# Gates of a hybrid encoder trunk: two of four contraction chunks as 2x2 Strassen products instead of one

## The chip, the cores and the metric

The kernel runs on one core of one Trainium2 chip. The metric is the device time of the whole launch in microseconds (us), the median of the runs. One execution was also recorded by the profiler; its trace is what the rows below come from. The engines are called PE (TensorE, matmuls), DVE (VectorE), ACT (ScalarE), POOL (GpSimd) and SP (SyncE, which only issues DMAs here).

## The reference, cut to what matters

Two layers of an encoder with 256 tokens and a width of 2048, all in float32. In each layer three attention branches are projected to 2048 columns and merged by sigmoid gates that are computed from the layer's input `x`:

```
ga, gb, gc = jnp.split(jax.nn.sigmoid(x @ w_gate[l] + b_gate[l]), 3, axis=-1)
mix = ga * (ya @ w_br_a[l]) + gb * (yb @ w_br_b[l]) + gc * (yc @ w_br_c[l])
x = layer_norm(DEEPNORM_ALPHA * x + mix @ w_out[l], ...)
f_gate, f_up = jnp.split(x @ w_ffn_in[l], 2, axis=-1)
x = layer_norm(DEEPNORM_ALPHA * x + (silu(f_gate) * f_up) @ w_ffn_out[l], ...)
```

`w_gate[l]` is 2048 x 6144. The change concerns the product `x @ w_gate[l]` only.

## The kernel before, in words

Every operand of a matmul is split into a high and a low part (`h`, `l`) of a reduced format, and every product of two float32 tiles is made of three matmuls, `h*wh`, `h*wl` and `l*wh`, each of 128 x 128 against 128 x 512, which accumulate in one PSUM bank. Weights come in *units*: 256 rows by 512 columns (two k tiles of 128 rows), 512 KB, loaded by SP into one of five buffers called `raw`. `split_unit` (L72 to L81) makes `wh` on ACT (L78) and then `wl` on DVE (L80), into six buffers each. The `raw` buffer is free once L80 has read it.

A plain `gemm` computes one block of 512 output columns for both halves of the tokens: a unit feeds 12 matmuls. `pair_gemm` (L317) computes two column blocks, `n1` and `n2`, at once, for the two token halves, with seven PSUM banks named `p1, p2, p3, p6, p7, q4, q5`. Four of them (`p3, q5, p7, q4`) come from the pool `psA` of four banks, which the plain gemms use too; three come from the pool `psX`. The contraction of 2048 has four chunks of 512 rows; each is done in one of these ways:

- `four(kt, c0)`: one unit of one column block, two products into two banks, 12 matmuls. A chunk takes four of them, 48 matmuls and four splits.
- `seven(c, fill)`: the chunk is a 2x2 block product by Strassen's method (Winograd's form). It loads four units (`hub`, `w22`, `w11`, `w21`), makes sums of them on DVE (L381, L389, L390, L403, each 128 x 1024) and does seven products of two k tiles each (`p7, p3, p1, q5, p6, p2, q4`), 42 matmuls and seven splits: those of `w22`, `w11`, `w21`, of the sum `hub`, and of the sum `u` three times. `fill` says which `four` calls stand between its products.

The sums on the token side are made once per layer by `x_sums` (L276) and reused by all pairs: for a `four` chunk one difference of 128 x 512 (L301) and one split, for a `seven` chunk four differences of 128 x 256 (L294, L295, L296, L298) and two splits. Their results live in twelve tiles named in `sum_tiles`, of which the gates use ten.

At the end of a pair (L452 to L467), DVE combines the seven banks and the bias of the gate (`bg`, loaded by POOL into a `raw` buffer) into four gate tiles; each of these operations is 128 x 512. Per layer the gates have six steps, three branches by two column pairs. The first step uses plain gemms; the other five call `pair_gemm`. Behind each come two plain gemms of the branch projection (eight k tiles each for branch a, four each for b and c) and on DVE L701, or L703 and L704, which multiply by the gate and add into `mix`.

The same `pair_gemm` serves the feed-forward layer, with `FF = ("7", "74", "4", "4")`, where `74` is a chunk of which half the rows go through seven products (`seven_half`).

The order of the work on each engine is fixed when the program is built, from the program's order and from the builder's own estimates; each engine then works through its list in order and waits on semaphores. In this list work of a later step can stand ahead of work of an earlier one.

Of the kernel before, what the change touches and what calls it, by code (L numbers as in the profile page):

```python
# [33 lines left out]
def trunk_kernel(ctx: ExitStack, tc: tile.TileContext, x, w_in, sinks, lq1, lk1, lq2, lk2, diff_g,  # L34
# [26 lines left out]
    def block(src, k0, c0):  # L61
        return src[k0 * P:(k0 + UK) * P, c0:c0 + CW].rearrange("(k p) n -> p k n", p=P)

    def load_raw(src, k0, c0):
        raw = wpool.tile([P, UK, CW], F32, tag="raw", name="raw", bufs=5)
        nc.sync.dma_start(raw, block(src, k0, c0))
        return raw
# [4 lines left out]
    def split_unit(raw):  # L72
        h = wpool.tile([P, UK, CW], F32R, tag="wh", name="wh", bufs=6)
        l = wpool.tile([P, UK, CW], F32R, tag="wl", name="wl", bufs=6)
        n = raw.shape[1]
        a, v = behind.pop(0) if behind else (None, None)
        with tc.issue_after(a) if a else nullcontext():
            nc.scalar.copy(h[:, 0:n], raw)  # L78
        with tc.issue_after(v) if v else nullcontext():
            split_ins.append(nc.vector.tensor_sub(l[:, 0:n], raw, h[:, 0:n].bitcast(F32)).ins)  # L80
        return h, l  # L81
# [128 lines left out]
    for layer in range(DEPTH):  # L210
# [106 lines left out]
        def pair_gemm(src, n1, n2, sums, kinds, load_bias=None, hubs=()):  # L317
# [19 lines left out]
            def prod(k, lhs, w, js=range(UK)):  # L337
                for i, j in enumerate(js):
                    (ah, al), (wh, wl) = lhs(i), w
                    nc.tensor.matmul(bank[k], ah, wh[:, j, :], start=k not in begun, stop=False)  # L340
                    begun.add(k)
                    nc.tensor.matmul(bank[k], ah, wl[:, j, :], start=False, stop=False)  # L342
                    todo[k] -= 1
                    nc.tensor.matmul(bank[k], al, wh[:, j, :], start=False, stop=todo[k] == 0)  # L344

            def part(h, l, j0):
                return lambda j: (h[:, j0 + j, :], l[:, j0 + j, :])

            def four(kt, c0):
                c, j0 = kt // 4, kt % 4  # L350
                a1, a2 = (part(xh[c][t], xl[c][t], j0) for t in range(NT))
                w = load_unit(src, kt, c0)
                if c0 == n2:
                    prod("q5", a2, w)
                    prod("p3", part(*sums[c][-1], j0 if kinds[c] == "4" else 0), w)
                else:
                    prod("p2", a1, w)
                    prod("q4", a2, w)
                units.append(w)
                if len(units) == 2:  # L360
                    run_later()
# [3 lines left out]
            def seven(c, fill):  # L365
                k1, k2 = 4 * c, 4 * c + 2
                a11, a12, a22 = (part(xh[c][t], xl[c][t], j) for t, j in ((0, 0), (0, 2), (1, 2)))
                s1, s2, s3, s4 = [part(h, l, j) for h, l in sums[c] for j in (0, 2)]

                def fours(i):  # L370
                    for f in fill[i]:
                        four(*f)

                if hubs:
                    hub = act.tile([P, UK, CW], F32, tag=hubs[c // 2], name="hub")
                    nc.sync.dma_start(hub, block(src, k1, n2))
                else:
                    hub = load_raw(src, k1, n2)
                w22 = load_raw(src, k2, n2)
                u = scr.tile([P, UK, CW], F32, tag="att", name="u", bufs=2)  # L380
                nc.vector.tensor_add(u, hub, w22)  # L381
                fours(0)
                prod("p7", s3, split_unit(u))
                prod("p3", s4, split_unit(w22))
                w11 = load_raw(src, k1, n1)
                if hubs:
                    nc.gpsimd.dma_start(hub, block(src, k1, n1), accum_op=ALU.add)
                else:
                    nc.vector.tensor_add(hub, hub, w11)  # L389
                nc.vector.tensor_add(u, u, w11)  # L390
                fours(1)
                prod("p1", a11, split_unit(w11))
                fours(2)
                if not hubs:
                    prod("q5", s1, split_unit(hub))
                    fours(3)
                prod("p6", s2, split_unit(u))
                w21 = load_raw(src, k2, n1)
                if hubs:
                    nc.gpsimd.dma_start(u, block(src, k2, n1), accum_op=ALU.add)  # L400
                    fours(3)
                else:
                    nc.vector.tensor_add(u, u, w21)  # L403
                fours(4)
                prod("p2", a12, split_unit(w21))
                if hubs:
                    prod("q5", s1, split_unit(hub))
                fours(5)
                prod("q4", a22, split_unit(u))
                fours(6)  # L410

            def seven_half(fill):
                b11, b12, b22 = (part(xh[1][t], xl[1][t], j) for t, j in ((0, 0), (0, 1), (1, 1)))
                s1, s2, s3, s4 = [part(*sums[1][0], j) for j in range(4)]
                w2 = load_raw(src, 4, n2)
                w1 = load_raw(src, 4, n1)
                u = scr.tile([P, 3, CW], F32, tag="att", name="u", bufs=2)
                nc.vector.tensor_add(u[:, 0], w2[:, 0], w1[:, 0])
                nc.vector.tensor_add(w2[:, 0], w2[:, 0], w2[:, 1])
                w = split_unit(w2)  # L420
                prod("p7", s3, w, (0,))
                prod("p3", s4, w, (1,))
                nc.vector.tensor_add(u[:, 1], u[:, 0], w2[:, 1])
                w = split_unit(w1)
                prod("p1", b11, w, (0,))
                prod("p2", b12, w, (1,))
                nc.vector.tensor_add(u[:, 2], u[:, 1], w1[:, 1])
                four(*fill[0])
                w = split_unit(u[:, 0:2])
                prod("q5", s1, w, (0,))  # L430
                prod("p6", s2, w, (1,))
                four(*fill[1])
                w = split_unit(u[:, 2:3])
                prod("q4", b22, w, (0,))

            N2, N1 = ([(k, c) for k in range(4, 16, 2)] for c in (n2, n1))
            if kinds[1] == "74":
                seven(0, [N2[1:2], N2[2:3], [], N2[3:4], [], [], []])
                seven_half(N2[4:])
                for f in N1[1:]:  # L440
                    four(*f)
            elif kinds[2] == "7":
                seven(0, [N2[0:1], N2[1:2], [], [], N2[4:5], N1[0:1], []])
                seven(2, [N2[5:6], N1[1:2], [], [], [], N1[4:], []])
            else:
                seven(0, [N2[0:1], N2[1:2], N2[2:3], N2[3:4], N2[4:], N1[0:1], N1[1:2]])
                if load_bias:
                    bias = load_bias()
                for f in N1[2:]:
                    four(*f)  # L450
# [208 lines left out]
        ys = [y0, y1, y2, y3]  # L659


        GATE = ("7", "4", "4", "4")
        FF = ("7", "74", "4", "4")
        mix = [[None] * NT for _ in range(NCH)]
        mixT = [None] * NCH
# [1 line left out]
        for b, (wbr, nk, y0i) in enumerate(((w_br_a, 8, 0), (w_br_b, 4, 2), (w_br_c, 4, 3))):  # L667
# [4 lines left out]
            for c0 in range(0, NCH, 2):  # L672
                cols = [b * D + c * CW for c in (c0, c0 + 1)]

                def load_bias(cols=cols):
                    t = wpool.tile([P, 2, CW], F32, tag="raw", name="bg", bufs=5)
                    for i, c in enumerate(cols):
                        nc.gpsimd.dma_start(t[:, i], b_gate[layer][c:c + CW].partition_broadcast(P))
                    return t[:, 0], t[:, 1]

                if b == 0 and c0 == 0:
                    bgs = load_bias()
                    side.append(x_sums(sums, GATE, 0))
                    gates = []
                    for c, bg in zip(cols, bgs):
                        acc = gemm(w_gate[layer], 0, 16, c, x_lhs)
                        gates.append([tmp("gate") for _ in range(NT)])
                        for t in range(NT):
                            nc.vector.tensor_add(gates[-1][t], acc[t], bg)
                    drain()  # L690
                else:
                    gates = pair_gemm(w_gate[layer], *cols, sums, GATE, load_bias)
                for gs in gates:
# [176 lines left out]
```

## Time and profile before

| | |
|---|---|
| median of 3 runs | 2802.61 us (2802.1 to 2805.56) |
| time of the profiled execution | 2802.2 us |
| its span, first to last instruction | 2800.4 us |
| PE busy | 2770.8 us, 99% |
| DVE busy | 2086.7 us, 75% |
| ACT busy | 1376.8 us, 49% |
| granted TensorE clock, mean | 0.999 |

Busy time is the time in which an engine works at least one instruction. Consecutive instructions overlap a little, so the mean duration of one is longer than the step from one start to the next. Between the span and the execution's time lie 1.8 us.

### The profile page before, as it was taken

What the parts mean: (1) busy time and instruction counts of PE and PEld (TensorE: products, weight loads), DVE (VectorE), ACT (ScalarE), POOL (GpSimd) and SP (SyncE); (2) the same over time, 40 slices, a digit from 0 to 9 for tenths busy, and PEclk for the clock granted to TensorE, in tenths of its full rate; (3) what the DMA queues carried; (4) which work ended last, traced back from release to release, by engine and by line L of the source; (5) the groups of instructions that cost most, each with busy time, mean ns of one, the idle gap of its engine ahead of it and who ended that gap; (6) DMA issues with size and microseconds to landing.
All of it is one profiled execution on the core that took longest, in us unless ns stands there. A gap on an engine that the chain in (4) does not pass through costs nothing. (4 is left out here: it accounts for less than half of the span.)

```text
span 2800.4 us, 33958 instructions
## 1 busy us (share of the span) xinstructions
PE 2770.8 (99%) x12600; PEld 2288.2 (82%) x12600; DVE 2086.7 (75%) x2438; ACT 1376.8 (49%) x1760; POOL 60.3 (2%) x110
## 2 busy tenths in 40 slices
PE   8999999999999999999999999999999999999998
PEld 7888888887888888888878888888878888888886
DVE  6665877776996698588676568787679957985886
ACT  4545544443554455455445455444435544553552
POOL 0000000000000000000000000000000000000000
PEclk9999999999999999999999999999999999999999
DMA  7556565674656566557564555666746655665573
GB/s 250 173 158 188 164 219 188 215 254 155 210 186 213 189 191 216 190 188 232 192 211 151 180 186 182 196 204 220 242 145 218 200 201 187 199 209 189 186 239 128
DMA packets 282663, 549.22 MB, mean 196 GB/s; under 512 B 19840, under 2 KB 21376, under 8 KB 282496
## 3 DMA queue, kind: packets, MB, share of 16 engines
q1 hardware_dynamic: 276096, 526.07, 57.7%
q0 software_dynamic: 6400, 20.98, 2.9%
q8 instruction: 99, 1.62, 0.2%
q14 instruction: 68, 0.56, 0.1%
HBM read 542.78 MB, written 4.19 MB: 195 GB/s over the span
## 5 line engine op out<-in xcount | busy, mean ns | idle before, releaser
L78 ACT CAST wh<-raw 128x1024 fp32r<-128x1024 f32 x992 | 1038.9, 1053 | 1192.2 <-PE acc L117 554.3
L80 DVE TENSOR_TENSOR wl<-raw,wh 128x1024 fp32r<-128x1024 f32 x992 | 1201.0, 1221 | 508.1 <-ACT wh L78 505.3
L115 PE MATMUL acc<-wh,rh 128*128 128x512 f32 x1216 | 475.3, 391 | 0.0
L117 PE MATMUL acc<-wh,rl 128*128 128x512 f32 x1216 | 473.8, 390 | 0.0
L116 PE MATMUL acc<-wl,rh 128*128 128x512 f32 x1216 | 473.4, 389 | 0.0
L115 PE MATMUL acc<-wh,xh 128*128 128x512 f32 x768 | 307.2, 401 | 0.0
L116 PE MATMUL acc<-wl,xh 128*128 128x512 f32 x768 | 300.7, 392 | 3.6 <-DVE wl L80 1.9
L117 PE MATMUL acc<-wh,xl 128*128 128x512 f32 x768 | 300.9, 392 | 0.0
L342 PE MATMUL q<-wl,xh 128*128 128x512 f32 x720 | 280.3, 389 | 2.6 <-DVE wl L80 2.6
L340 PE MATMUL q<-wh,xh 128*128 128x512 f32 x720 | 280.3, 389 | 0.0
L344 PE MATMUL q<-wh,xl 128*128 128x512 f32 x720 | 280.1, 389 | 0.0
L117 PEld LDWEIGHTS acc<-wh,rl 128*128 128x128 f32 x1216 | 228.3, 188 | 47.3
L115 PEld LDWEIGHTS acc<-wh,rh 128*128 128x128 f32 x1216 | 228.3, 188 | 46.8
L116 PEld LDWEIGHTS acc<-wl,rh 128*128 128x128 f32 x1216 | 228.3, 188 | 46.7
L340 PE MATMUL p<-wh,sums 128*128 128x512 f32 x560 | 218.1, 389 | 0.7 <-DVE v L703 0.7
L344 PE MATMUL p<-wh,sums 128*128 128x512 f32 x560 | 218.0, 389 | 0.0
L342 PE MATMUL p<-wl,sums 128*128 128x512 f32 x560 | 217.9, 389 | 0.0
L340 PE MATMUL p<-wh,xh 128*128 128x512 f32 x480 | 188.4, 392 | 0.0
L344 PE MATMUL p<-wh,xl 128*128 128x512 f32 x480 | 186.9, 389 | 0.0
L342 PE MATMUL p<-wl,xh 128*128 128x512 f32 x480 | 186.8, 389 | 0.0
L116 PEld LDWEIGHTS acc<-wl,xh 128*128 128x128 f32 x768 | 144.5, 188 | 34.2 <-DVE wl L80 4.1
L117 PEld LDWEIGHTS acc<-wh,xl 128*128 128x128 f32 x768 | 144.2, 188 | 31.6 <-DVE xl L55 1.3
(208 smaller groups left out, 3110.1 us busy)
## 6 DMA issues: line engine op xcount, KB each, us to landing
raw<-in_w_ffn_in_dram SPq DMA_DIRECT2D x352, 512.0 KB, 4.3
raw<-in_w_gate_dram SPq DMA_DIRECT2D x192, 512.0 KB, 4.4
raw<-in_w_ffn_out_dram SPq DMA_DIRECT2D x176, 512.0 KB, 3.7
raw<-in_w_in_dram SPq DMA_DIRECT2D x144, 512.0 KB, 3.8
raw<-in_w_out_dram SPq DMA_DIRECT2D x64, 512.0 KB, 4.3
raw<-in_w_br_a_dram SPq DMA_DIRECT2D x32, 512.0 KB, 4.7
raw<-in_w_br_b_dram SPq DMA_DIRECT2D x16, 512.0 KB, 5.6
raw<-in_w_br_c_dram SPq DMA_DIRECT2D x16, 512.0 KB, 5.4
```

What stands on the lines that cost most here:

```text
L78: nc.scalar.copy(h[:, 0:n], raw)
L80: split_ins.append(nc.vector.tensor_sub(l[:, 0:n], raw, h[:, 0:n].bitcast(F32)).ins)
L115: nc.tensor.matmul(acc[t], ah, wh[:, j, :], start=kt == 0, stop=False)
L116: nc.tensor.matmul(acc[t], ah, wl[:, j, :], start=False, stop=False)
L117: nc.tensor.matmul(acc[t], al, wh[:, j, :], start=False, stop=kt == nk - 1)
L340: nc.tensor.matmul(bank[k], ah, wh[:, j, :], start=k not in begun, stop=False)
L342: nc.tensor.matmul(bank[k], ah, wl[:, j, :], start=False, stop=False)
L344: nc.tensor.matmul(bank[k], al, wh[:, j, :], start=False, stop=todo[k] == 0)
```

## The change

`GATE` names how each of the four chunks of the contraction is done in the gates. Chunk 2 becomes a `seven` as well. `pair_gemm` then takes its middle branch, in which the `fill` lists hold the remaining eight `four` calls, and the bias of the gate is loaded between the two `seven` calls instead of behind the first.

```
             elif kinds[2] == "7":
                 seven(0, [N2[0:1], N2[1:2], [], [], N2[4:5], N1[0:1], []])
+                if load_bias:
+                    bias = load_bias()
                 seven(2, [N2[5:6], N1[1:2], [], [], [], N1[4:], []])
             else:
                 seven(0, [N2[0:1], N2[1:2], N2[2:3], N2[3:4], N2[4:], N1[0:1], N1[1:2]])
...
-        GATE = ("7", "4", "4", "4")
+        GATE = ("7", "4", "7", "4")
         FF = ("7", "74", "4", "4")
```

`N2[i]` and `N1[i]` are the `four` units of the column blocks `n2` and `n1` at k tile 4 + 2i. `x_sums` follows `GATE`, so its chunk 2 takes the `seven` form, and all twelve tiles are used.

## Rows read from the trace of the kernel before

**Rows 1.** The page's first part (engines over the span) and TensorE's clock, in 40 slices.

```profile
PE 2770.8 (99%) x12600; PEld 2288.2 (82%) x12600; DVE 2086.7 (75%) x2438; ACT 1376.8 (49%) x1760; POOL 60.3 (2%) x110
...
PEclk9999999999999999999999999999999999999999
```

**Rows 2.** Waits of PE, whole span: us in total, times, longest.

```profile
PE q L342 <- DVE wl L80: 2.6, 2, 1.3
...
PE p L340 <- DVE v L703: 0.7, 1, 0.7
```

**Rows 3.** Timeline of PE: first matmul of layer 0's second pair, first behind it.

```profile
381.15 0.39 PE L340 MATMUL q<-wh,xh 128*128 128x512 f32 x1
...
423.31 0.39 PE L115 MATMUL acc<-wh,rh 128*128 128x512 f32 x1
```

**Rows 4.** Windows: first pair; steps (pair, branch gemms); four feed-forward pairs; layer 1's steps.

```profile
core 0: us, PE busy (x) PEld busy (x) DVE busy (x) ACT busy (x) POOL busy (x), PEclk, DMA share, GB/s
315.60:359.40 43.80, 42.52 (x188) 34.76 (x187) 37.35 (x40) 22.52 (x23) 1.07 (x2) 1.00 0.69 233
...
381.20:434.20 53.00, 53.00 (x236) 43.88 (x235) 39.42 (x42) 26.47 (x27) 1.06 (x2) 1.00 0.63 201
434.20:487.30 53.10, 53.10 (x236) 43.88 (x235) 41.32 (x45) 26.48 (x27) 1.07 (x2) 1.00 0.63 202
487.30:542.30 55.00, 54.26 (x243) 44.45 (x242) 43.28 (x47) 27.17 (x28) 1.06 (x2) 1.00 0.64 208
542.30:597.50 55.20, 55.20 (x254) 45.88 (x253) 44.63 (x51) 28.18 (x32) 6.40 (x12) 1.00 0.83 264
951.80:1120.40 168.60, 168.60 (x757) 139.85 (x756) 148.35 (x160) 93.12 (x100) 0.00 (x0) 1.00 0.64 202
1771.60:1824.60 53.00, 53.00 (x236) 43.90 (x234) 40.48 (x43) 26.24 (x27) 1.07 (x2) 1.00 0.64 206
1824.60:1877.60 53.00, 53.00 (x235) 43.93 (x234) 42.00 (x45) 26.56 (x27) 1.06 (x2) 1.00 0.65 208
1877.60:1931.50 53.90, 53.90 (x244) 44.71 (x243) 43.03 (x47) 26.97 (x28) 1.07 (x2) 1.00 0.64 206
1931.50:1986.00 54.50, 54.50 (x249) 45.23 (x248) 42.94 (x49) 27.60 (x32) 6.40 (x12) 1.00 0.81 262
```

**Rows 5.** Lines by form, whole span: the two halves of a split.

```profile
L80 DVE TENSOR_TENSOR wl<-raw,wh 128x1024 fp32r<-128x1024 f32 x992 | 1201.0, 1221 | 508.1 <-ACT wh L78 505.3
L78 ACT CAST wh<-raw 128x1024 fp32r<-128x1024 f32 x992 | 1038.9, 1053 | 1192.2 <-PE acc L117 554.3 <-PE q L344 173.8 <-PE p L344 171.3
```

**Rows 6.** Timeline of DVE in layer 0's first pair: start, us, instruction (xN: N merged).

```profile
303.25 0.42 DVE L294 TENSOR_TENSOR zs<-z 128x256 f32<-128x256 f32 x1
303.59 0.17 DVE L500 RECIPROCAL rc<-sm 128x4 f32<-128x4 f32 x1
...
316.75 1.27 DVE L701 TENSOR_TENSOR mix<-gate,acc 128x512 f32<-128x512 f32 x2
317.94 0.68 DVE L55 TENSOR_TENSOR sums<-z,sums 128x512 fp32r<-128x512 f32 x1
...
321.95 5.75 DVE L80 TENSOR_TENSOR wl<-raw,wh 128x1024 fp32r<-128x1024 f32 x5
327.63 1.22 DVE L80 TENSOR_TENSOR wl<-u,wh 128x1024 fp32r<-128x1024 f32 x1
```

**Rows 7.** Waits of DVE, layer 0's second to fourth gate steps, 381.2 to 542.3.

```profile
DVE p L456 <- DMA bg<-in_b_gate_dram: 11.2, 3, 3.9
DVE u L381 <- DMA raw<-in_w_gate_dram: 10.8, 3, 4.0
DVE raw L389 <- DMA raw<-in_w_gate_dram: 8.7, 3, 3.1
```

**Rows 8.** Waits of DVE, four feed-forward pairs, 951.8 to 1120.4.

```profile
DVE u L381 <- DMA raw<-in_w_ffn_in_dram: 1.3, 2, 0.9
DVE u L418 <- DMA raw<-in_w_ffn_in_dram: 0.8, 1, 0.8
```

More of the change, by code (lines that the diff above doesn't have):

```diff
@@ L443, in pair_gemm @@
                 seven(0, [N2[0:1], N2[1:2], [], [], N2[4:5], N1[0:1], []])
+                if load_bias:
+                    bias = load_bias()
                 seven(2, [N2[5:6], N1[1:2], [], [], [], N1[4:], []])
@@ L659, in trunk_kernel @@
         ys = [y0, y1, y2, y3]
-        GATE = ("7", "4", "4", "4")
+        GATE = ("7", "4", "7", "4")
         FF = ("7", "74", "4", "4")
```

## The prediction

> **What bounds the kernel now.** I read the page first: PE is busy for 99% of the span at a clock of 0.9 or more in every slice, DVE for 75% [rows 1]. So time falls only with PE's work, as long as nothing else takes the bound. Then the waits of PE: in the gates and everywhere else they are crumbs, yet the crumbs name what comes next. Two waits of up to 1.3 us are for `wl`, a split that DVE made late, and one of 0.7 us is for DVE's L703, which frees a PSUM bank that the next pair's `p7` needs [rows 2]. Then the timeline for the price of a matmul: between the first matmul of a pair and the first one behind it lie 423.31 - 381.15 = 42.16 us [rows 3]. A pair has 186 matmuls (42 of `seven`, 12 x 12 of `four`), which makes 0.2267 us each, without a gap. Last the windows by step, to see how much of DVE's time each step leaves [rows 4]: a gate step behind the first takes 53 to 55 us, of which DVE works 39 to 45; four feed-forward pairs take 168.6 us, of which DVE works 148.35, 88%, with PE busy throughout.
>
> **The change part by part.**
>
> *Matmuls removed.* A pair goes from 42 + 144 = 186 to 2 x 42 + 8 x 12 = 180. Five pairs in each of two layers: 60 matmuls fewer, 60 x 0.2267 = 13.6 us, or 1.36 us a pair. PE is the bound there, so all of it counts as long as DVE keeps up.
>
> *DVE work added.* A pair goes from 19 splits (7 + 12) to 22 (14 + 8) and from four block sums to eight. All seven operations are 128 x 1024. The mean duration is 1.22 us [rows 5], but what a full queue pays is the step from start to start: five in a row from 321.95 to 327.63, 1.136 us each [rows 6]. So 7 x 1.136 = 7.95 us a pair. Is there room? The eight steps of pairs 2 to 5 in both layers take 430.7 us with DVE busy for 337.1 (sums of eight windows of [rows 4], 78%). After: 337.1 + 8 x 7.95 = 400.7 us of DVE in 430.7 - 8 x 1.36 = 419.8 us, 95%. The cover is 19 us, 2.4 us a step. So the added work lies beside the matmuls, but nearly without reserve; without cover it would cost 80 us for ten pairs.
>
> What this says of each queue: behind a late DVE operation stand the splits that PE waits for, L456 to L466 that empty the pair's banks, and L701 to L704 that free the banks for the next pair. The six `wl` buffers let splits run ahead of PE, by six units of 6 or 12 matmuls (8 to 16 us). The banks have less: `p7` is needed 12 matmuls (2.7 us) into a pair, and there the 0.7 us wait of today stands.
>
> *Does DVE wait for loads?* In gate steps 2 to 4 it does, for 11.2 us at the bias, 10.8 at L381 and 8.7 at L389 over three steps, 10.2 us a step [rows 7]. If the second `seven` brought its own 3.6 + 2.9 us, the 2.4 us of room would be gone. In the feed-forward, where DVE is at 88%, the same kind of wait is 1.3 + 0.8 = 2.1 us in four pairs, 0.5 a pair, none at L389 [rows 8]. The bounds are therefore 0.5 and 13 us a pair (twice 6.5, bias left out). I take 1 to 2: the loads are the same 16 units a pair, a buffer comes free whenever a split ends, and a DVE with a backlog reaches L381 later. At 95% the gates are nearer to the feed-forward's rows than to those at 78%.
>
> *The bias.* Its two POOL instructions are issued earlier, between the two `seven`. L456, which needs the last product of `p1`, then comes at least 9.5 us behind it (the 42 matmuls from the second `seven`'s start to the end of `p1`), so the 3.7 us wait goes. It hides in DVE's spare time today and PE doesn't gain by it; it is part of the room above. In exchange `bg` holds one of five `raw` buffers through the whole second `seven`, and SP's queue has four. I price that at nothing, between nothing and one L389 wait (2.9 us a pair); what is late next would be `w11`.
>
> *Token sums.* Chunk 2 takes four operations of 128 x 256 for one of 128 x 512, and a second split. Steps: 0.34 us for the small ones and 0.595 for the large [rows 6]. 4 x 0.34 - 0.595 + 0.595 = 1.36 us a layer on DVE and one more cast of half a split on ACT. They stand ahead of the first pair's splits, where DVE is already late: the first pair takes 43.80 us with PE busy for 42.52 [rows 4], and this is where the waits of 1.3 us lie. No cover, so it is charged in full: 2 x 1.4 = 2.8 us. Bounds: nothing (if the builder puts them behind) and 3 us a layer (sums plus half of the first pair's further DVE work).
>
> *ACT and the end of the pair.* Three casts more, 3 x 1.05 = 3.2 us [rows 5], on an ACT busy for 26 to 28 of 53 us [rows 4]: hidden. `p6` now ends with `p2`, two `four` and `q4` to go, 36 matmuls or 8.2 us; before, 108 matmuls followed it. In this time DVE must do L458, L459, L460, L462 and L463, 5 x 0.595 = 3 us, before the branch gemm has two banks. Hidden unless four or five splits stand between, 5.7 us more; then the banks come 0.5 us late.
>
> *PSUM banks.* A busier DVE reaches L703 and L463 later. Today one of eight starts waits 0.74 us. Bounds for the average: nothing and 1.4 us (two splits ahead of it that are not there today, less the slack of the other starts). I take 0.5, as the queue is fuller but not over-full: 8 x 0.5 = 4.0 us.
>
> *Sum.* 2802.2 us for the profiled execution - 13.6 + 2.8 + 4.0 = 2795.4. The median of the runs lies 0.4 us above that execution, which gives **2795.8 us**, a gain of 6.8.
>
> **A rule against the change.** The step of 1.136 us stands below the duration of 1.22: the next DVE operation starts before the last has ended [rows 5, 6]. The Trainium skill, "VectorE: DVE Perf Modes", section Terms (DRAIN), says that the next operation can't issue until the pipe has emptied. By that rule each would cost its whole duration. A step has 30 + 4 = 34 operations of 1024 columns and some 18 of 512; their overlap is 34 x 0.085 + 18 x 0.085 = 4.4 us, and the step's 50.1 us of DVE would become 54.5, over PE's 52.5. The trace speaks against it, five steps of 1.136 in a row.
>
> **The rivals.**
> *A: all of it arrives.* The builder hides the token sums and no bank is late: 2802.6 - 13.6 = 2789, with today's waits perhaps 2788.5. For it: 5% of room and the feed-forward without waits at 88%. Against: the first pair has no room today.
> *B: bank waits eat the gain.* If L703 or L463 comes 0.7 to 1.4 us late at each of ten pairs, 7 to 14 us are lost beside the token sums' 2.8: 2802.6 - 13.6 + 2.8 + 7 or 14, 2799 to 2806. For it: the 0.74 us wait of today, in a step with 10 us of spare DVE time, so the queue's order alone can do it.
> *C: DVE becomes the bound, slower.* One mechanism: each `seven` waits at L381 and L389 for its loads, with `bg` in a fifth of the buffers. It decides where the waits exceed the room of 2.4 us plus the 1.36 us saved: 3.8 us a pair, 1.9 a `seven`. At 3.3 us a `seven`, half of today's 6.5, a pair loses 6.6 - 2.4 = 4.2 us: 8 x 4.2 - 13.6 + 2.8 = +23, 2825 us. Against: feed-forward's 0.5 us a pair.
> *D: operations that don't overlap.* Every step 54.5 against 53.8 us today, 8 x 0.7 + 2.8 = +8: 2811 us.
> That fewer matmuls are not issued is no rival: the counts follow from the code.
>
> **How the numbers follow.** 0.2% is 5.6 us, about what a measurement of this kernel tells from no change. My forecast holds as a case from 2793 to 2798.5: chance 0.45. A 0.12, B 0.22, C 0.19, D 0.02. Faster by over 0.2% (below 2797): four fifths of the forecast and A, 0.48. Within 0.2%: the rest of the forecast and B, 0.31. Slower: C and D, 0.21. The range has to leave out no more than 0.2: it begins at A's 2788.5 and ends at 2808, where B and the lightest part of C lie; what is above is most of C and D, 0.17, and 0.02 lie below. The likeliest case's own range is 2793 to 2798.5.
>
> **What the profile would show.** PE: 12540 matmuls, a step from first to last of 180 x 0.2267 = 40.8 us in undisturbed pairs. DVE: 70 more operations of 128 x 1024 (seven in each of ten pairs), near 95% busy in the gate steps; L456's wait for `bg` gone; L381 and L389 waits for `w_gate` under 2 us a pair. PE's waits for `wl` in the first pair of each layer at some 2.7 instead of 1.3 us; waits for L703, L463 or L464 at pair starts and branch gemms of some 4 us in all. The prediction is wrong if DVE waits for loads over 3.8 us a pair (C), if PE's bank waits reach 1.4 us a pair (B), or if both stay as they are (A).

## The result and the profile after

The changed kernel takes 2828.72 us (2827.38 to 2829.92), the kernel before 2803.2 us on the same chip: a ratio of 1.0095, 95% interval 1.0083 to 1.0108. It is slower by 0.95%, outside the range and on the other side of the forecast. The profiled execution took 2827.56 us, its span is 2825.8 us, 25.4 us more than before.

In the changed kernel's code the lines behind the new bias load stand two further down: L458 adds the bias, L460 to L468 combine the banks, L703 and L705 multiply by the gate. What was L458 in the prediction is L460 here. The page's first line, engines over the span; it answers to [rows 1]:

```profile
PE 2771.8 (98%) x12540; PEld 2280.9 (81%) x12540; DVE 2165.0 (77%) x2516; ACT 1400.2 (50%) x1792; POOL 60.3 (2%) x110
```

60 matmuls are gone, as counted, and DVE is busy for 78.3 us longer, near the 82 us counted. But PE is busy for as long as before, in part because some matmuls run at half clock (last section), and it has idle time. Its waits over the whole span, against [rows 2] (us in total, times, longest):

```profile
PE acc L115 <- DVE c L465: 13.9, 10, 1.9
PE p L340 <- ACT wh L78: 5.0, 3, 2.4
...
PE acc L115 <- DVE v L462: 4.1, 4, 1.5
...
PE p L342 <- DVE wl L80: 2.3, 4, 0.8
```

The waits at L465 and L462 are new. L465 reads `p7` and L462 reads `q5` for the last time; both banks come from `psA`, and the branch gemm behind the pair (L115) needs two banks of it. The wait for L465 stands behind every one of the ten pairs. Second come the splits, in the first and the fifth pairs.

The windows by step, layer 0 (first pair, then four steps of pair and branch gemms), against [rows 4]:

```profile
core 0: us, PE busy (x) PEld busy (x) DVE busy (x) ACT busy (x) POOL busy (x), PEclk, DMA share, GB/s
314.70:359.70 45.00, 41.96 (x182) 33.36 (x181) 42.01 (x44) 22.09 (x23) 1.11 (x2) 1.00 0.59 191
382.60:435.80 53.20, 52.05 (x230) 42.76 (x229) 46.31 (x48) 28.45 (x30) 1.06 (x2) 1.00 0.59 192
435.80:491.60 55.80, 53.79 (x230) 43.78 (x229) 50.41 (x53) 28.56 (x30) 1.07 (x2) 0.97 0.60 198
491.60:545.80 54.20, 52.73 (x236) 43.43 (x235) 50.51 (x54) 28.96 (x31) 1.06 (x2) 1.00 0.64 205
545.80:610.60 64.80, 58.18 (x245) 46.02 (x244) 51.90 (x57) 30.43 (x35) 7.44 (x14) 0.95 0.73 241
```

The fifth step went from 55.2 to 64.8 us; the others should be 1.36 us shorter, and the best of them is 0.8 us shorter. From first to last the five steps took 281.9 us in layer 0 and 280.0 in layer 1 before (597.5 - 315.6 and 1986.0 - 1705.96), and take 295.9 and 290.3 now (610.6 - 314.7 and 2010.0 - 1719.7): 24.3 of the span's 25.4 us are here.

Where they come from, read from start to start of the matmuls in the timeline over both layers: the saving, -13.6; bank waits behind the ten pairs, 20.6; waits for splits in the fifth pairs, 6.8; in the first pairs 2.54 us where there were 1.44, +2.2; the bank wait of before is gone, -0.7; and stretches at half clock, 17.1 us that cost half, +8.5. The sum is 23.8. The saving itself is there: pairs 2 to 4 take 40.8 us to the first matmul behind them, 180 x 0.2267, where they took 42.16 [rows 3]; only the third of layer 0 takes 0.3 us more. The loss lies right behind them.

The end of the third pair, DVE's timeline (start, us, instruction):

```profile
469.50 0.68 DVE L458 TENSOR_TENSOR p<-p,bg 128x512 f32<-128x512 f32 x1
470.11 1.22 DVE L80 TENSOR_TENSOR wl<-u,wh 128x1024 fp32r<-128x1024 f32 x1
471.24 1.22 DVE L80 TENSOR_TENSOR wl<-raw,wh 128x1024 fp32r<-128x1024 f32 x1
472.37 0.68 DVE L460 TENSOR_TENSOR v<-p,p 128x512 f32<-128x512 f32 x1
472.98 1.21 DVE L80 TENSOR_TENSOR wl<-raw,wh 128x1024 fp32r<-128x1024 f32 x1
474.11 0.68 DVE L461 TENSOR_TENSOR y<-p,v 128x512 f32<-128x512 f32 x1
474.86 1.23 DVE L80 TENSOR_TENSOR wl<-raw,wh 128x1024 fp32r<-128x1024 f32 x1
476.00 0.68 DVE L462 TENSOR_TENSOR v<-q,v 128x512 f32<-128x512 f32 x1
476.60 1.22 DVE L80 TENSOR_TENSOR wl<-raw,wh 128x1024 fp32r<-128x1024 f32 x1
477.74 0.69 DVE L464 TENSOR_TENSOR v<-v,bg 128x512 f32<-128x512 f32 x1
478.34 0.68 DVE L467 TENSOR_TENSOR p<-p,p 128x512 f32<-128x512 f32 x1
478.94 0.68 DVE L465 TENSOR_TENSOR c<-v,p 128x512 f32<-128x512 f32 x1
```

and PE's, at the same place (idle time before it and its releaser in brackets):

```profile
477.38 0.40 PE L117 MATMUL acc<-wh,rl 128*128 128x512 f32 x1
479.67 0.55 PE L115 MATMUL acc<-wh,rh 128*128 128x512 f32 x1 [1.90 <-DVE c L465]
```

L458, L460, L461, L462, L464 and L465 form a chain: each uses what an earlier link wrote, or writes over what the link before it still reads (L462 over `v`, which L461 reads). Splits of the next units stand between them. A link with one split behind it takes 0.6 + 1.14 = 1.74 us; between L458 and L460 stand two splits. The whole runs from 469.50 to 479.62, 10.1 us. PE wants `p7`'s bank at 477.38 + 0.23 = 477.61 and gets it 2.06 us late.

DVE's waits over the second to fourth steps, against [rows 7]:

```profile
DVE wl L80 <- ACT wh L78: 7.6, 11, 2.6
DVE u L381 <- DMA raw<-in_w_gate_dram: 4.2, 3, 2.0
DVE bg L459 <- DMA bg<-in_b_gate_dram: 2.1, 1, 2.1
...
DVE raw L389 <- DMA raw<-in_w_gate_dram: 0.2, 1, 0.2
```

DVE itself waits for unit loads for 1.5 us a step, no more than was forecast. But L80 waits for ACT, and ACT waits for the loads too.

### The profile page after: what moved, and what is told of

The parts are those of the page before. It is cut to its first block, busy times and chain, and to the rows that moved or that the text cites. A ratio compares the mean times of both kernels' runs of the same rounds, so it can differ in the third digit from the quotient of the medians.

```text
span 2825.8 us, 33972 instructions
## 1 busy us (share of the span) xinstructions
PE 2771.8 (98%) x12540; PEld 2280.9 (81%) x12540; DVE 2165.0 (77%) x2516; ACT 1400.2 (50%) x1792; POOL 60.3 (2%) x110
## 4 chain that ended last, share of the span: by engine, by line
PE 40%; DVE 5%; DMA 3%; issue 1%; ACT 1%; DVEq 0%; ACTq 0%
PE acc L115 8%; PE acc L117 8%; PE acc L116 8%; PE p L342 3%; PE p L344 3%; PE p L340 3%; DVE wl L80 3%; PE q L344 2%; PE q L342 2%; PE q L340 2%; DMA raw<-in_w_gate_dram 2%; ACT wh L78 1%; DMA raw<-in_w_br_b_dram 0%; PE hidTp L166 0%; DVE r L741 0%
## 5 line engine op out<-in xcount | busy, mean ns | idle before, releaser
L80 DVE TENSOR_TENSOR wl<-raw,wh 128x1024 fp32r<-128x1024 f32 x992 | 1201.7, 1221 | 513.2 <-ACT wh L78 511.5
L115 PE MATMUL acc<-wh,rh 128*128 128x512 f32 x1216 | 480.0, 395 | 18.1 <-DVE c L465 13.9
L115 PE MATMUL acc<-wh,xh 128*128 128x512 f32 x768 | 307.4, 401 | 0.1
L115 PEld LDWEIGHTS acc<-wh,rh 128*128 128x128 f32 x1216 | 229.9, 189 | 71.4 <-DVE c L465 18.2
L342 PE MATMUL q<-wl,xh 128*128 128x512 f32 x660 | 257.5, 390 | 1.5 <-DVE wl L80 1.5
L340 PE MATMUL q<-wh,xh 128*128 128x512 f32 x660 | 257.7, 390 | 1.0 <-ACT wh L78 0.9
L344 PE MATMUL q<-wh,xl 128*128 128x512 f32 x660 | 257.5, 390 | 0.0
L340 PE MATMUL p<-wh,sums 128*128 128x512 f32 x580 | 226.5, 391 | 4.7 <-ACT wh L78 4.7
L342 PE MATMUL p<-wl,sums 128*128 128x512 f32 x580 | 226.6, 391 | 0.0
L344 PE MATMUL p<-wh,sums 128*128 128x512 f32 x580 | 226.3, 390 | 0.0
L80 DVE TENSOR_TENSOR wl<-u,wh 128x1024 fp32r<-128x1024 f32 (+1 forms) x160 | 184.2, 1151 | 2.6 <-ACT wh L78 2.0
L78 ACT CAST wh<-u 128x1024 fp32r<-128x1024 f32 (+1 forms) x160 | 159.7, 998 | 53.4 <-PE p L344 18.5
```

Of the source, the lines that this page charges most:

```text
L115: nc.tensor.matmul(acc[t], ah, wh[:, j, :], start=kt == 0, stop=False)
```

## The experiments

Ratios are against the kernel before on the same chip, with their 95% intervals. Four theories were in play: the *tail* (too few matmuls behind `p6` to cover the chain), the *load* (DVE too full, wherever the work stands), the *bias buffer* (`bg` takes one of five `raw` buffers up to the end of the pair, unit loads start late, and all DVE work, the chain too, loses its lead), and the *collision* (the layer norm's broadcast loads, issued by POOL, land in the fifth pair and slow the unit loads).

**The load alone.** The kernel before, in which the low half of each split of the one `seven` is made twice, seven operations more a pair:

```
+        if again:
+            nc.vector.tensor_sub(l[:, 0:n], raw, h[:, 0:n].bitcast(F32))
...
-                prod("p7", s3, split_unit(u))
+                prod("p7", s3, split_unit(u, bool(load_bias)))
...
```

> The kernel before the change, with DVE's load of the change alone: in each gate pair the seven splits of the one seven chunk do L80 twice (7 x 1.136 = 7.95 us a pair, the output is the same). Rival 'load': PE waits as in the changed kernel, 2803 + 20 to 27 = 2823 to 2830. Theory 'tail': 108 matmuls (24 us) follow p6, the combination still hides; less than 5 us lost, 2803 to 2808.

2808.52 us, ratio 1.0024 (1.0013 to 1.0035). Third step:

```profile
437.00:490.10 53.10, 53.10 (x236) 43.94 (x235) 49.88 (x53) 26.43 (x27) 1.06 (x2) 1.00 0.63 208
```

DVE works for 94% of the third step and PE waits for nothing. The 6 us stand mostly in the first pairs, which take 47.0 and 46.5 us instead of 43.8 each: 4.8 us of waits for `wl` at their `p` products, and two stretches of 3.4 us at half clock. The load alone is not the cause.

**The tail.** Four of the eight `four` units go behind the second `seven`:

```
-                seven(0, [N2[0:1], N2[1:2], [], [], N2[4:5], N1[0:1], []])
+                seven(0, [N2[0:1], N2[1:2], [], [], N2[4:5], [], []])
...
-                seven(2, [N2[5:6], N1[1:2], [], [], [], N1[4:], []])
+                seven(2, [N2[5:6], [], [], [], [], [], []])
+                for f in N1[0:2] + N1[4:]:
+                    four(*f)
```

> The changed kernel with the same work in another order: the four units of n1 (48 matmuls) stand behind the second seven instead of between its products, so that 60 matmuls follow p6's last product and not 36. Theory 'tail': the changed kernel loses 20.6 us where the branch gemm waits for the banks of q5 and p7 (L462, L465), plus some 7 us of half clock behind these waits, because the combination of the banks shares DVE's list with splits and has 8.2 us of matmuls to hide behind; with 13.6 us it hides, the bank waits fall under 3 us and the time falls by 20 to 27 us to 2802 to 2809. Rival 'load': DVE at 95% is late wherever it is asked; the waits move to wl inside the pair and the time stays within 5 us of 2828.7.

2827.03 us, 1.0088 (1.0071 to 1.0104), no gain. The chain has more cover: its end (L467 there) still makes five waits, but of 3.7 us in all. PE now waits more for what stands later in DVE's list (L470 here is L468 in the changed kernel, the last combination, and L707 is L705, the gate multiply):

```profile
PE acc L115 <- DVE y L470: 9.8, 6, 2.5
PE p L340 <- DVE v L707: 6.7, 4, 1.7
```

So DVE's list is late as a whole, not the chain alone. As a full account the tail theory fell.

**The chain written earlier**, directly behind `p6`'s product:

```
                 prod("p6", s2, split_unit(u))
+                if c == 2:
+                    combine()
```

> The changed kernel with the order of fills kept; L458 to L466, all of the combination that doesn't need p2 and q4, stand in the program right behind p6's last product, ahead of the splits of the units that follow, so the builder gives them precedence. Theory 'tail': DVE's list no longer alternates chain and splits, q5's and p7's banks come free some 5 us earlier, the bank waits (20.6 us) fall to under 5 us: 2803 to 2810. Rival 'load': the splits are late instead, within 5 us of 2828.7. A third way: the list was ruled by p6's end and not by the program's order, then nothing changes.

2825.16 us, 1.0081 (1.0066 to 1.0096). The builder's list still alternates links and splits, and the longest bank waits stay at 2.07 us. Program order didn't move the chain, so this tells nothing on what a denser chain would give.

**A shorter chain.** `c22` is made from `q5` plus bias and `y`, so that `p7` is free after three links:

```
+                nc.vector.tensor_sub(y, bank["p7"], v)
+                nc.vector.tensor_add(c22, bank["q5"], bias[1])
+                nc.vector.tensor_add(v, v, c22)
+                nc.vector.tensor_sub(c22, c22, y)
```

> The changed kernel with the same ten operations per gate pair, three of them written otherwise, so that the banks come free earlier: q5 plus bias is made by itself and the last quarter is that sum minus y, so p7's bank is free after three dependent operations (L458, L460, L461) instead of six, and q5's needs none of them. Theory 'chain': the six links each cost 1.74 us (0.6 and a split in between), 9 to 11 us against 8.2 us of matmuls; with three links the bank waits of 20.6 us and the 6.8 us of half clock behind them go, 2803 to 2809 remain (fifth pairs 6.8 us, first pairs 2.6 us stay). Rival 'late list': DVE's list as a whole runs late there, the wait moves to p3's or q4's bank or to wl, as in e1: within 8 us of 2828.7.

2822.48 us, 1.0069 (1.0054 to 1.0084). The waits at L115 in the gates are gone, 20 us of them, and 7 us are gained: the starts of the next pairs wait instead (3.7 us for L708, which is L705 in the changed kernel and frees a bank), and the fifth pairs take 51.6 and 54.0 us where the changed kernel takes 48.2 and 46.5. The lateness moves on to whatever PE needs next.

**The bias a second `seven` later**, with the shorter chain:

```
                 seven(0, [N2[0:1], N2[1:2], [], [], N2[4:5], N1[0:1], []])
+                seven(2, [N2[5:6], N1[1:2], [], [], [], N1[4:], []])
                 if load_bias:
                     bias = load_bias()
-                seven(2, [N2[5:6], N1[1:2], [], [], [], N1[4:], []])
```

> The early bank release with the bias loaded behind the second seven instead of between the two. Rival 'four buffers': with all five raw buffers in the second seven the waits for loads (first and fifth pairs) shrink, 3 to 6 us below the run with the early release alone. Theory 'shared queues': within 2 us of it, or slower where the first link now waits for the bias.

2820.47 us, 1.0065 (1.005 to 1.008), not to be told from the shorter chain alone. The bias still takes a `raw` buffer, now from 460.5 to 478.2 us in the third step, 17.7 us where it was 33.7 with the shorter chain alone. The fifth pairs take 10.9 us less together, but pairs 2 to 4 take 4.7 us more and part of the rest comes back behind the fifth pairs.

**No bias load in pairs 2 to 5**; the bias operations read a tile that is there, so this kernel leaves the bias out of those gates:

```
                 def load_bias(cols=cols):
+                    if not (b == 0 and c0 == 0):
+                        t = xh[0][0].rearrange("p k q -> p (k q)").bitcast(F32)
+                        return t, t
...
```

> The changed kernel without the gates' bias loads in the pairs: the same ten DVE operations, but with tokens of the input in the bias's place (so the bias is left out of the gates), five raw buffers in the second seven and no load on POOL there. Rival 'four buffers': the waits for loads in the fifth pairs (11 us with half clock) and part of the late combination go, 2812 to 2820. Theory 'shared queues': the fifth pair keeps its waits, 2825 to 2829.

2809.3 us, 1.0029 (1.0017 to 1.0041): some 18 us of the 26 are gone with one buffer's use, while DVE does the same operations. Pairs 2 to 4 run without a PE wait, 40.8 us and 10.9 for the branch (11.7 behind the fourth, which holds transposes too).

**The bias in a buffer of its own.** The whole computation is kept; `bg` of pairs 2 to 5, eight of the ten, goes into a tile that is free at that time:

```
+                    if b == 0:
+                        t = wpool.tile([P, 2, CW], F32, tag="raw", name="bg", bufs=5)
+                    else:
+                        t = act.tile([P, 2, CW], F32, tag=f"rh{2 * b - 2}", name="bg")
```

> The changed kernel with the bias of pairs 2 to 5 loaded into a tile that is free then (a branch's token tile, same size) instead of one of the five raw buffers; the bias is complete. Theory 'four buffers': as in the run without bias, pairs 2 to 4 and their branch gemms run undisturbed (11 us of bank waits with half clock go), the fifth pair keeps the waits that the layer norm's loads make: 2808 to 2818. Rival 'the bias load itself': the broadcast load takes the queues' time wherever it lands: within 3 us of 2828.7.

2810.68 us, 1.0031 (1.002 to 1.0042), as without the bias. Third to fifth steps:

```profile
435.60:487.30 51.70, 51.70 (x229) 42.79 (x228) 50.09 (x53) 29.31 (x30) 0.00 (x0) 1.00 0.63 204
487.30:539.80 52.50, 52.50 (x238) 43.55 (x236) 50.91 (x55) 29.78 (x31) 2.13 (x4) 1.00 0.67 222
539.80:601.00 61.20, 56.38 (x241) 45.09 (x239) 50.90 (x55) 30.01 (x34) 6.38 (x12) 0.94 0.74 238
```

With DVE busy for 97% of the third step PE is busy for all of it: 51.7 us against 53.1 before, the 1.36 us saved. The chain is the same, and its link still takes 1.74 us; here it is in the third pair, DVE's timeline without the splits between:

```profile
466.62 0.69 DVE L458 TENSOR_TENSOR p<-p,bg 128x512 f32<-128x512 f32 x1
...
469.49 0.68 DVE L460 TENSOR_TENSOR v<-p,p 128x512 f32<-128x512 f32 x1
...
471.22 0.68 DVE L461 TENSOR_TENSOR y<-p,v 128x512 f32<-128x512 f32 x1
...
475.98 0.68 DVE L465 TENSOR_TENSOR c<-v,p 128x512 f32<-128x512 f32 x1
```

L465 ends at 476.66, 41.1 us after the step's start at 435.6; in the changed kernel it is 479.62 - 435.8 = 43.8 us. PE wants the bank at 477.11 - 435.6 = 41.5 us here and at 477.61 - 435.8 = 41.8 us there. So the chain has 0.4 us to spare if DVE is on time, and 2 us are missing if its list is 2.7 us late. The links behind `p6` take as long in both, 7.2 us from L460's start to L465's end (472.37 to 479.62 and 469.49 to 476.66); what differs is when L460 starts. The last matmul of `p6`, which L460 reads, stands at the same place of the pair, in the changed kernel (first line) and with the bias in its own tile (second):

```profile
468.18 0.39 PE L344 MATMUL p<-wh,sums 128*128 128x512 f32 x1
...
468.04 0.39 PE L344 MATMUL p<-wh,sums 128*128 128x512 f32 x1
```

L460 starts 4.2 us behind it in the one and 1.5 us in the other. That lead is what the buffer takes. SP's timeline shows how: loads of the third step (start, us from first to last, xN: N merged), in the changed kernel

```profile
439.79 22.79 SPq L66 DMA_DIRECT2D raw<-in_w_gate_dram  x9
463.34 6.64 SPq L66 DMA_DIRECT2D raw<-in_w_br_b_dram  x4
```

and with the bias in its own tile

```profile
439.32 17.51 SPq L66 DMA_DIRECT2D raw<-in_w_gate_dram  x9
457.60 7.63 SPq L66 DMA_DIRECT2D raw<-in_w_br_b_dram  x4
```

The same nine loads take 22.8 us to be issued instead of 17.5, and the branch weights start 27.5 us into the third step instead of 22.0. From 384 to 480 us, twelve casts on ACT wait 25.7 us for their loads, against five with 8.8 us.

How long the buffer was gone is in POOL's timeline, in the third step of the kernel before (first line) and of the changed one (last line); the line between is the last reader of `bg` before, and in the changed kernel that is L464 at 477.74, shown above:

```profile
445.75 1.07 POOL L678 DMA_DIRECT2D bg<-in_b_gate_dram  x2 [52.56 <-DVE wl L80]
...
459.28 0.69 DVE L462 TENSOR_TENSOR v<-v,bg 128x512 f32<-128x512 f32 x1
...
441.19 1.07 POOL L680 DMA_DIRECT2D bg<-in_b_gate_dram  x2 [57.40 <-DVE wl L80]
```

Though the program loads the bias between the two `seven`, POOL issues it 5.4 us into the step, and `bg` holds its buffer for 37.2 us instead of 14.2.

**The layer norm's loads, three tries that did not move them.** In the fifth pair POOL issues the eight broadcast loads of the layer norm's gain and shift (L727), from 551.6 to 573.0 us in layer 0. Before, six of them stood there and two at 265.6 us: these two use the tag `bc`, of whose four buffers the token sums held two and hold all four since all twelve sum tiles are in use. So the change itself moved two loads into this pair, as POOL's counts of the step show, 14 instead of 12 [rows 4]. The loads were written later in the program, and then held back by an ordering hint:

```
-        lnp = norm_params(ln1_g[layer], ln1_b[layer])
...
+            if c == 0:
+                lnp = norm_params(ln1_g[layer], ln1_b[layer])
```

> The changed kernel with the 8 broadcast loads of the layer norm's parameters issued behind the first w_out gemm instead of during the fifth pair. Theory 'shared queues': the fifth pair's waits for wh and wl (6.8 us over both layers) come from these loads, which land with the gates' units in 7 to 10 us instead of 4.5; without them they go and the time falls by 5 to 8 us to 2821 to 2824. Rival 'four buffers': the bias holds one of five raw buffers in the second seven, and the fifth pair waits anyway: within 2 us of 2828.7.

```
+                if c == 0 and t == NT - 1:
+                    with tc.issue_after(bn.ins):
+                        lnp = norm_params(ln1_g[layer], ln1_b[layer])
```

> The changed kernel with the layer norm's 8 broadcast loads held back until the first w_out block is done (in e4 the builder had moved them back to the fifth pair, so e4 tested nothing). Theory 'shared queues': the gates' units of the fifth pair land in 4 to 5 us instead of 7 to 10, the waits of that pair (4.3 and 2.6 us, and some half clock) go: 2819 to 2823. Rival 'own loads': the second seven makes these waits with its four raw buffers: within 2 us of 2828.7.

The second of these edits together with the shorter chain:

> Both of the edits above, the early bank release and the loads held back. If the two causes add: 2795 to 2803 us, at or below the kernel before, with the first pairs' 2.5 us each left. Rival 'DVE full at 95%': other waits take their place, over 2810.

2825.74 us, 1.0089 (1.0073 to 1.0104); 2829.85 us, 1.0097 (1.0082 to 1.0112); 2819.39 us, 1.0064 (1.0047 to 1.008). In all three POOL still issues the loads in the fifth pair, six of them from 550 to 559 us in the first. They are inconclusive on the collision and show only that the place of a load in the program doesn't fix when POOL issues it.

**The loads held back by data.** Their tiles get one column written by DVE from the first block of the output gemm, so that the load must wait for it:

```
+                if behind_tile is not None:
+                    nc.vector.tensor_copy(t[:, 0:1], behind_tile[:, 0:1])
                 nc.gpsimd.dma_start(t, v[c * CW:(c + 1) * CW].partition_broadcast(P))
```

> The changed kernel with the layer norm's 8 loads really held back: each tile first gets one column from DVE out of the first w_out block, and the load writes over it (in e4 and e6 the trace shows these loads still issued inside the fifth pair, so neither tested it). Theory 'shared queues': the fifth pair's units land in 4 to 6 us, its waits (11 us in the two layers with their half clock) go: 2817 to 2821. Rival 'four buffers': within 2 us of 2828.7.

2818.56 us, 1.0054 (1.0038 to 1.007). The fifth pairs fall from 48.2 and 46.5 us to 43.7 and 41.8; the bank waits stay. In the changed kernel's fifth pair the landing of unit loads, against its third pair, by the view of the tile `raw` (first line: fifth pair, second: third):

```profile
DMA to landing us min/median/max: 7.1/9.4/10.2
...
DMA to landing us min/median/max: 3.7/5.2/6.7
```

and DVE's timeline in the fifth pair:

```profile
564.61 1.23 DVE L381 TENSOR_TENSOR u<-raw 128x1024 f32<-128x1024 f32 x1 [4.16 <-DMA raw<-in_w_gate_dram]
568.34 1.22 DVE L80 TENSOR_TENSOR wl<-raw,wh 128x1024 fp32r<-128x1024 f32 x1 [2.50 <-ACT wh L78]
```

With the loads held back units land here in a median of 6.4 us, and with the bias in its own tile as well in 4.4. Before, six of the eight loads stood in this step, with a DMA share of 0.83; units took up to 10.1 us and ACT waited 11.8 us for them, but PE had no wait there [rows 4]. DVE had ten spare microseconds in that step; that these were the cover fits the rows, but no run takes them away alone.

**Combinations.** Shorter chain and held loads:

> The early release of the banks and the loads held back as in e10. With the early release alone the fifth pairs take 51.6 and 54.0 us instead of 42.4 (188 matmuls and transposes undisturbed), so theory 'shared queues' gives 2822.5 less 15 to 20: 2802 to 2807, about the kernel before. Rival 'four buffers': within 3 us of 2822.5.

2805.3 us, 1.0012 (1.0004 to 1.0021). Bias in its own tile and held loads, and nothing else changed, the chain as it is:

> The bias away from the raw buffers and the layer norm's loads held back behind the first w_out block; the combination of the banks as in the change. If these two are the cause, only the first pairs' 2.5 us each and their clock are left of the loss: 2789 + 2 x 4 = 2797, between 2794 and 2801, faster than the kernel before. If the combination's chain is a cause of its own, the bank waits stay and the time is over 2808.

2796.74 us, 0.9981 (0.9972 to 0.999). The fifth step, and PE's waits from 300 to 600 us:

```profile
537.80:591.40 53.60, 53.60 (x248) 44.58 (x246) 51.66 (x56) 31.36 (x35) 2.13 (x4) 1.00 0.71 234
```

```profile
PE p L340 <- ACT wh L78: 2.4, 1, 2.4
PE acc L115 <- DVE c L465: 0.8, 1, 0.8
PE acc L115 <- DVE v L462: 0.5, 1, 0.5
```

All three waits left belong to the first pair. With the shorter chain as well:

> The same with the early release of the banks. If the chain of six links has no cost once the loads are in time: within 2 us of the run without it. If it does: 3 to 8 us less.

2793.13 us, 0.997 (0.9958 to 0.9982): 3.6 us less, about the bank waits that the run before had left behind the first pairs. And with chunk 2's token sums made between the two `seven` of the first pair instead of ahead of it:

```
+                while rest:
+                    for _ in rest.pop():
+                        pass
...
+                    side.append(x_sums(sums, GATE, 0, (0, 1, 3), shared))
+                    rest.append(x_sums(sums, GATE, 0, (2,), shared))
```

> The same again with the token sums of chunk 2 made between the two sevens of the first pair instead of ahead of it. The first pair's wait of 2.54 us and the 3.4 us of half clock behind it come from DVE being late at its start: with 3.8 us of DVE work less there they fall below the kernel before's 1.4 us: 3 to 7 us less than the run with late sums left out, 2789 to 2794. If the wait comes from the order of the first seven's own sums (L389, L390 ahead of the split), it stays: within 1 us.

2788.21 us, 0.9952 (0.9939 to 0.9964), the fastest of all kernels here; a mean clock of 0.999, and no wait of over 1.1 us in the gates:

```profile
PE 2756.7 (99%) x12540; PEld 2277.0 (82%) x12540; DVE 2164.1 (78%) x2532; ACT 1405.7 (50%) x1792; POOL 60.3 (2%) x110
```

As a control, the kernel before with the bias in its own tile, the held loads and the shorter chain, but one `seven`:

> The kernel before, one seven, with the three edits that need no second seven: bias away from the raw buffers, the layer norm's loads held back, early release of the banks. Its PE waits in the gates are 3 us a layer at most. If the second seven is what makes the last version faster, this one stays at 2799 to 2803. If the edits themselves bring the gain, it comes under 2796.

2802.14 us, 1.0002 (0.9993 to 1.0011). Those three edits give nothing by themselves; what they give to the changed kernel is what the second `seven` had lost. The fourth, the late token sums, has no counterpart there.

## Why the prediction was wrong

**The matmuls removed, -13.6 us: right.** Undisturbed pairs take 40.8 us, 1.36 us less. The kernel without the side effects comes out 0.48% below the one before, 13.5 us of 2802; that this is so near is in part chance, as it also lost the 1.3 us waits that the first pairs had before.

**DVE's work beside the matmuls: right.** It is 96 to 97% busy in undisturbed steps and PE waits for nothing. Rival D falls with it: three splits in a row fill 3.50 us in the trace of after, less than 3 x 1.22 = 3.66. The Trainium skill, "VectorE: DVE Perf Modes", Terms (DRAIN), says that the next operation can't issue until the pipe has emptied; that again doesn't show in these independent operations.

**Waits for loads, 1 to 2 us a pair: right as a number** (4.4 us in three steps), **wrong as the place to look.** Most of the lateness goes through ACT's casts to L80.

**The bias, "I price that at nothing": the step that failed.** Taking `bg` out of the `raw` buffers is worth 1.0095 - 1.0031 = 0.64%, 18 us, or 2.2 us for each of the eight pairs in which it was done. My own upper bound of 2.9 us a pair held it; I chose nothing without a row for it. The wait that shows, 2.1 us at L459 in three steps, says little of the price: four buffers instead of five make the unit loads, and with them DVE's list, late, by 2.7 us in the third pair. Before, `bg` took a buffer too, and taking it out, with two more edits, gives nothing there (the control): the buffer costs only where DVE is full. How the cost goes with the time held stays open, as the run with 17.7 instead of 33.7 us gained nothing.

**The end of the pair, 3 us, "Hidden unless four or five splits stand between": mis-sized, and the reason not met.** The five links behind `p6` (L460 to L465 here) take 7.2 us, not 3, as the builder puts a split behind most of them. With DVE on time that is still hidden, with 0.4 us to spare; there was no cover for the 2.7 us by which L460 came late.

**Bank waits, 0.5 us at each of eight, 4.0 in all: mis-sized and misplaced.** They are 2.06 us at each of ten on average, 20.6 in all, and at L465 and L462 in front of the branch gemm, not at the gate multiply. The prediction's own sign for rival B, 1.4 us a pair, was passed.

**Token sums, 2.8 us: about right by the waits, low by the run.** The first pairs wait 1.1 us longer in each layer, 2.2 in all; moving the sums gains 0.18% more, about 5 us, by medians, and the first pairs' wait of 2.4 us is gone, with the half clock that can follow it.

**Not in the sum:** the collision with the layer norm's loads, 1.0095 - 1.0054 = 0.41%, 11.5 us alone; with the bias away as well, 1.14% or 32 us for both. That all twelve sum tiles would be in use was known, but not that this holds two of these loads back into the fifth pair; what these two cost of the 11.5 us no run shows. And the clock, 8.5 us by the rows, which comes and goes with the waits and is thus part of these differences.

**Rival C** had the time, 2825 us, and its cause, `bg` in a fifth of the buffers. Its mechanism, waits of over 3.8 us a pair at L381 and L389, is not what happens: they are 1.5. What C missed is that an engine at 95% needs no long wait to become late, and that PE feels it at the banks.

With the bias and the layer norm's loads out of the way the kernel takes 2796.74 us, close to the 2795.8 forecast. That is in part luck: the forecast held 4.0 us of bank waits at eight later starts, and what is left of waits there stands in the first pairs.

Left open: why the builder alternates the chain with splits, and what a chain without splits between would give; writing it earlier didn't produce one.

## What to carry to other kernels

When a change fills an engine to 95%, ask what each moved small load holds: a buffer taken from the weight stream can delay the loads behind it, and here the lateness came out where the engine's list frees something that PE needs, more than where the load is awaited. Price a chain of dependent operations on a full engine at its links plus whatever the list puts between them. And look at which transfers of the next stage land in the stretch that just lost its slack.

## What the runs showed of the hardware

TensorE's clock fell to its lower level, 1.2 GHz, behind some of the new waits. Windows of the changed kernel, first the wait behind the third pair, then what follows:

```profile
476.80:479.90 3.10, 1.16 (x4) 0.71 (x5) 3.10 (x5) 0.63 (x1) 0.00 (x0) 1.00 0.84 296
480.00:483.40 3.40, 3.40 (x9) 2.65 (x8) 3.40 (x5) 2.70 (x5) 0.00 (x0) 0.50 0.80 290
483.40:490.00 6.60, 6.60 (x30) 5.45 (x29) 5.08 (x7) 3.74 (x4) 0.00 (x0) 1.00 0.24 79
```

Nine matmuls stand where 3.40 us at full clock hold 15, and a wait of 1.9 us cost another 1.7 us. There are four such stretches in the gates, three of 3.4 us and one of 6.9 us behind the fifth pair's two waits of 1.5 and 1.9 us (596.0 to 602.9, granted clock 0.51). But the same wait of 1.9 us for L465 at 1938.5 us, in layer 1, left the clock at 1.00, and of the two first pairs' waits of 2.4 us only that of layer 1 was followed by half clock (1729.3 us), so a short wait doesn't always cost it. The Trainium skill, "TensorE: Matmul & The Clock Gate", Part 1, says that the throttled clock is the default and activity releases it. The rows here agree in so far as the clock in the gates fell only behind idle time.
